# Reciprocal roots of the first norm and of the indexer key's norm: a power on GpSimd and one Newton step in place of a seed and three steps

## The chip, the cores and the metric

The kernel runs on one core of a Trainium2 chip. The metric is the device time of one execution in microseconds (us). The engines of the core work side by side and meet at semaphores: TensorE (PE in the profile, its weight loads PEld) multiplies matrices, VectorE (DVE) and ScalarE (ACT) work element by element and can read the matmul results, GpSimd (POOL) works element by element on the on-chip memory alone, and SyncE (SP) issues most transfers.

## The reference

Two decoder layers over 512 tokens of width 1024, in float32. A layer norm stands in front of the layers. Each layer projects the tokens to the queries, keys and values of two attention groups (a sliding window of 128 with sinks, and a sparse one) and to an indexer that picks, for each query, the 128 best keys of the sparse group. The attention results are projected back, and a norm of the weighted sum follows; then a gated feed-forward block with a gated per-layer input, and a norm again.

What matters here is the layer norm:

```
mu  = x.mean(-1);  var = square(x - mu).mean(-1)
y   = (x - mu) * rsqrt(var + 1e-5) * g + b
```

It is computed on the input x (512 x 1024, "the first norm"), on the indexer's keys (512 x 32, once a layer, "the indexer key's norm"), and twice a layer on the residual stream.

## The kernel before

The tokens lie on the 128 partitions in four tiles (t = 0 to 3), each 128 x 1024. For a projection a tile is turned to features by TensorE transposes (L438); ScalarE copies the result to a high part `fh` (L440, reduced float32) and VectorE puts the rest in a low part `fl` (L441). Weights are split the same way: ScalarE makes the high part (L278), GpSimd subtracts it to get the low part (L279). A product is then three matmuls, high x high (L325), high x low of the weights (L326) and low x high (L327), summed in one bank.

The order of each engine's work is set by a planner: the framework simulates a timeline and gives each engine, at each moment, the earliest instruction in program order of those that are ready. `tc.issue_after(i)` adds the demand that what is traced in its block comes after instruction i on i's engine. Each engine then runs its list in that order.

The start-up works tile by tile. `ln_in(t)` is the first norm. Tile 0's mean and variance are VectorE's (L372, L392); for tiles 1 to 3 ScalarE sums the tile (L382), scales the sum (L383) and sums the squares (L377). VectorE subtracts the mean and multiplies by g (L397, two halves), takes the reciprocal root with `rstd_of`, and multiplies by it and adds b (L400, two halves). The program then turns the tile to features and projects it to the indexer's query, key and weights (`gi_out`, 296 columns). Beside this GpSimd and ScalarE build the tables of the rotary embedding: `rotary` reduces the angles in two passes, each with a rounding on GpSimd (L462, L463), products on ScalarE (L473) and subtractions on GpSimd (L477), six in the first pass and four in the second. The rotations (L511 on VectorE, L513 on GpSimd, then a split L516 and L517) need the tables.

`rstd_of` is VectorE's alone. L357 adds epsilon to the variance and scales it by -0.5, L358 makes a seed from the bits of the number, and three Newton steps follow, each with two operations for each column: L363 (t = s * s * v) and L364 (s = (t + 1.5) * s). For the first norm the operands are 128 x 1. For the indexer key's norm two token tiles go together (128 x 2): the scaling and the seed are one operation each, the steps are twelve. Its statistics are L562 and L563, its first fused operation L564, and L580 applies the root. The pair's keys are then rotated, split and transposed for the indexer's scores (L645), whose weighted sum VectorE makes (L648). The two norms on the residual stream use `rstd_of` too.

Of the kernel before, what the change touches and what calls it, by code (L numbers as in the profile page):

```python
# [10 lines left out]
F32 = mybir.dt.float32  # L11
# [4 lines left out]
OP = mybir.AluOpType  # L16
# [13 lines left out]
EPS = 1e-5  # L30
# [66 lines left out]
def hybrid_kernel(ctx: ExitStack, tc: tile.TileContext, x, p, positions, ln_in_g, ln_in_b, w_in,  # L97
# [3 lines left out]
    PE, V, A, G, SP = nc.tensor, nc.vector, nc.scalar, nc.gpsimd, nc.sync  # L101
# [6 lines left out]
    small = ctx.enter_context(tc.tile_pool(name="small", bufs=4))  # L108
# [10 lines left out]
    def slot(dt=F32R):  # L119
        return slots.tile([128, 512], dt, name="slot", tag="slot")  # L120

    def t2k(dt=F32):
        return tmp.tile([128, 512], dt, name="t2k", tag="t2k")

    def sm(n, name):
        return small.tile([128, n], F32, name=name, tag=name)
# [222 lines left out]
        return slice(t * 128, (t + 1) * 128)  # L349


    def rstd_of(var, n=1, of=1):

        v = sm(n, f"lnv{n}")
        s = sm(n, f"lns{n}")
        t = sm(n, f"lnt{n}")
        V.tensor_scalar(v, var, of * EPS, -0.5 / of, op0=OP.add, op1=OP.mult)  # L357
        V.tensor_scalar(s.bitcast(I32), v.bitcast(I32), -0.5, float(0x5F3759DF - 2 ** 30 - 2 ** 22),  # L358
                        op0=OP.mult, op1=OP.add)
        for _ in range(3):  # L360
            for i in range(n):
                c = slice(i, i + 1)
                V.tensor_scalar(t[:, c], s[:, c], s[:, c], v[:, c], op0=OP.mult, op1=OP.mult)  # L363
                V.tensor_scalar(s[:, c], t[:, c], 1.5, s[:, c], op0=OP.add, op1=OP.mult)  # L364
        return s

    stats, last = {}, {}

    def ln_stats(t, h):
        if h == 0:  # L370
            stats[t] = small.tile([128, 2, 6], F32, name="bst", tag="bst")
        V.bn_stats(stats[t][:, h, :], xt[t][:, h * 512:(h + 1) * 512])  # L372
# [13 lines left out]
    def ln_in(t):  # L386
        halves = [xt[t][:, h * 512:(h + 1) * 512] for h in range(2)]
        if t == 0:
            mv = sm(2, "bmv")
            for h in range(2):  # L390
                ln_stats(t, h)
            V.bn_aggr(mv, stats.pop(t))  # L392
            mean, var, of = mv[:, 0:1], mv[:, 1:2], 1
        else:
            (mean, var), of = stats.pop(t), D
        for h, c in enumerate(halves):
            V.scalar_tensor_tensor(c, c, mean, gb_in[h], op0=OP.add if t else OP.subtract, op1=OP.mult)  # L397
        rs = rstd_of(var, of=of)
        for h, c in enumerate(halves):
            last["norm"] = V.scalar_tensor_tensor(c, c, rs, gb_in[2 + h], op0=OP.mult, op1=OP.add).ins  # L400

# [46 lines left out]
    def split_bits(v, bits):  # L448
        e = math.floor(math.log2(abs(v)))
        q = 2.0 ** (e - bits + 1)  # L450
        return math.floor(v / q) * q

    def rotary():

        n = NT * 48
        ang, kk, aa = t2k(), t2k(), t2k()
        a3 = ang[:, :n].rearrange("p (t f) -> p t f", t=NT)
        G.tensor_tensor(a3, posf[:, :, None].to_broadcast([128, NT, 48]),
                        invf[:, None, :].to_broadcast([128, NT, 48]), OP.mult)
        magic = 1.5 * 2.0 ** 23  # L460
        for period, bits, terms in ((2 * math.pi * 4096, 7, 6), (2 * math.pi, 11, 4)):
            G.tensor_scalar(kk[:, :n], ang[:, :n], 1.0 / period, magic, op0=OP.mult, op1=OP.add)  # L462
            G.tensor_scalar(kk[:, :n], kk[:, :n], magic, 1.0, op0=OP.subtract, op1=OP.mult)  # L463
            rest = period
            products = []
            for i in range(terms):
                c = split_bits(rest, bits) if i < terms - 1 else float(np.float32(rest))
                rest -= c
                if i % 2 == 0:
                    pr = t2k()  # L470
                products.append(pr[:, i % 2 * n:i % 2 * n + n])
                with tc.issue_after(last["squares"]) if bits == 11 else nullcontext():
                    A.mul(products[-1], kk[:, :n], -c)  # L473
            if bits == 7:
                yield
            for pr in products:
                G.tensor_tensor(ang[:, :n], pr, ang[:, :n], OP.add)  # L477
        lim = 3.1415925
        G.tensor_scalar(ang[:, :n], ang[:, :n], lim, -lim, op0=OP.min, op1=OP.max)
        with tc.issue_after(last["squares"]):  # L480
            A.activation(aa[:, :n], ang[:, :n], AF.Sin)
            A.activation(kk[:, :n], ang[:, :n], AF.Sin, scale=0.5)
        G.tensor_tensor(kk[:, :n], kk[:, :n], kk[:, :n], OP.mult)
        G.tensor_scalar(kk[:, :n], kk[:, :n], -2.0, 1.0, op0=OP.mult, op1=OP.add)
        s3 = aa[:, :n].rearrange("p (t f) -> p t f", t=NT)
        c3 = kk[:, :n].rearrange("p (t f) -> p t f", t=NT)
        for tab, f0, h in ((tab64, 0, 32), (tab32, 32, 16)):
            A.copy(tab[:, :, 0, :h], c3[:, :, f0:f0 + h])
            A.copy(tab[:, :, 0, h:], c3[:, :, f0:f0 + h])
            A.copy(tab[:, :, 1, :h], s3[:, :, f0:f0 + h])  # L490
            G.tensor_scalar(tab[:, :, 1, h:], s3[:, :, f0:f0 + h], -1.0, 1.0, op0=OP.mult, op1=OP.mult)

    w_pump()
    ln_in(0)
    table = rotary()
    next(table)
    ln_in_sums(1)
# [21 lines left out]
    def turn(dst, src, n):  # L519

        ps = bank("tp", 2, F32R)
        for i in range(n):
            PE.transpose(ps[:, i * 128:(i + 1) * 128], src[:, i * 128:(i + 1) * 128], idr)  # L523
        A.copy(dst, ps[:, :n * 128])
# [23 lines left out]
    for l in range(L):  # L548
# [6 lines left out]
        def gi_out(t, ps):  # L555

            u = t % 2
            if u == 0:
                kin[t] = sm(2 * ID, "kin").rearrange("p (u d) -> p u d", u=2)
                kmv[t] = sm(4, "kmv").rearrange("p (u d) -> p u d", u=2)  # L560
            st = sm(6, "kst6")
            V.bn_stats(st, ps[:, 256:288])  # L562
            V.bn_aggr(kmv[t - u][:, u], st)  # L563
            V.scalar_tensor_tensor(kin[t - u][:, u], ps[:, 256:288], kmv[t - u][:, u, 0:1], ikg[:, l],  # L564
                                   op0=OP.subtract, op1=OP.mult)
            qs = []
            if t > 0:
                wi[t] = small.tile([128, IH], F32, name="wi", tag="wi", bufs=4)
                V.tensor_scalar(wi[t], ps[:, 288:296], IH ** -0.5 * ID ** -0.5, None, op0=OP.mult)
                qs = [slot(), slot()]  # L570
                r1 = ps[:, :256].rearrange("p (n d) -> p n d", n=IH)
                for j in range(2):
                    qv = qs[j].rearrange("p (n u s d) -> p n u s d", n=4, u=2, s=2)
                    rope(r1[:, 4 * j:4 * j + 4], t, 4, ID, qv[:, :, :, 0], qv[:, :, :, 1], 2, top=G.tensor_copy)
            if u == 1:
                t0 = t - 1
                kn, mv = kin[t0], kmv[t0]
                rs = rstd_of(mv[:, :, 1], 2)
                for i in range(2):
                    V.scalar_tensor_tensor(kn[:, i], kn[:, i], rs[:, i:i + 1], ikb[:, l], op0=OP.mult, op1=OP.add)  # L580
                ks = slot()
                iv = ks[:, :256].rearrange("p (t s u d) -> p t s u d", t=2, s=2, u=2)
                rope(kn, t0, 2, ID, iv[:, :, 0], iv[:, :, 1], 2, each=True, top=G.tensor_copy)

            def turns():
                if u == 1:
                    turn(kiT[:, t0 * 128:(t + 1) * 128], ks, 2)
                    ready.add(("ki", t0))
                for j, q in enumerate(qs):
                    qiT[t, j] = slot()  # L590
                    turn(qiT[t, j], q, 4)
                ready.add(("i", t))
                order.tick(0.6)
            order.later(D_GI if t < NT - 1 else D_KI, turns)
# [370 lines left out]
        for gi, fs in enumerate(GROUPS):  # L965
# [27 lines left out]
            for h in range(2):  # L993
                ps = [acc() for _ in range(NT)]
                n = len(hs)
# [72 lines left out]
```

## Time and profile before

| | us |
|---|---|
| median of 3 runs | 1251.45 |
| lowest and highest | 1251.43, 1251.7 |
| profiled execution | 1251.81 |
| its span, first to last instruction | 1249.7 |

| engine | busy us | share of the span |
|---|---|---|
| TensorE | 1225.9 | 98% |
| its weight loads | 1029.9 | 82% |
| VectorE | 765.2 | 61% |
| GpSimd | 682.9 | 55% |
| ScalarE | 576.4 | 46% |

A busy share is an average over the whole span; TensorE's is modelled, as matmuls overlap in its pipeline. A row of a timeline has its start in us from the span's start, its duration in us, engine, source line, operation, output and inputs with shapes, and how many like it were merged; in brackets stands the idle time of the engine before it and what ended it. Rows that overlap on one engine are pipelined.

### The profile page before, as it was taken

The page shows a single profiled execution, that of the slowest core. Times are in us where ns is not written, and L with a number is a line of the kernel's source. Part 1 is how long each engine was busy: PE and PEld are TensorE (multiplying, and loading weights), DVE is VectorE, ACT ScalarE, POOL GpSimd, SP SyncE. Part 2 cuts the span into 40 slices and gives each one's busy share as a digit, 9 for nine tenths or more (in the row PEclk, how much of TensorE's full clock was granted, in tenths as well). Part 3 has the DMA queues.
Part 4 walks back from the last instruction along what each step waited for, and adds up shares of the span by engine and source line. Part 5 has one row for each costly group of instructions (what it writes and reads, how often), then busy time and mean ns, then how long its engine had stood idle before and what let it go on. Part 6 is the DMA issues. An engine that isn't in the chain of part 4 may idle for free.

```text
span 1249.7 us, 18006 instructions
## 1 busy us (share of the span) xinstructions
PE 1225.9 (98%) x6552; PEld 1029.9 (82%) x6552; DVE 765.2 (61%) x1678; ACT 576.4 (46%) x1193; POOL 682.9 (55%) x555
## 2 busy tenths in 40 slices
PE   7999999999999999999999999999999999999996
PEld 5998777988888888888899987689888888888885
DVE  7699954682727272726677998286555555555365
ACT  6577763442434343433337787534343333333331
POOL 6885532566566666663169754234757575757400
PEclk9999999999999999999999999999999999999999
DMA  5232311333232323034033203114323333321321
GB/s 177 78 92 85 95 42 35 119 118 118 85 118 84 118 85 118 18 118 140 2 89 114 101 21 117 52 54 149 99 87 105 97 105 99 103 83 52 101 84 50
DMA packets 89264, 112.74 MB, mean 90 GB/s; under 512 B 5460, under 2 KB 66132, under 8 KB 89176
## 3 DMA queue, kind: packets, MB, share of 16 engines
q1 hardware_dynamic: 88504, 111.58, 28.5%
q8 instruction: 51, 0.84, 0.3%
q14 instruction: 37, 0.30, 0.1%
q10 hardware_dynamic: 672, 0.03, 0.0%
HBM read 109.49 MB, written 2.10 MB: 89 GB/s over the span
## 4 chain that ended last, share of the span: by engine, by line
PE 82%; POOL 5%; DVE 3%; issue 3%; ACT 3%; DMA 3%; SPq 0%; DVEq 0%; ACTq 0%; POOLq 0%
PE bank L325 24%; PE bank L326 24%; PE bank L327 24%; PE bank L715 3%; PE bank L684 3%; PE bank L721 2%; POOL wsp L279 2%; DMA wst<-in_w_pg_dram 2%; POOL wsp L257 1%; PE bank L523 1%; PE bank L438 1%; PE bank L732 1%; ACT wsp L278 1%; DVE slot L273 1%; POOL slot L517 1%
## 5 line engine op out<-in xcount | busy, mean ns | idle before, releaser
L279 POOL TENSOR_TENSOR wsp<-wst,wsp 128x1024 fp32r<-128x1024 f32 (+2 forms) x148 | 351.3, 2389 | 244.4 <-ACT wsp L278 240.8
L326 PE MATMUL bank<-fl,wsp 128*128 128x512 f32 (+1 forms) x768 | 284.8, 372 | 0.4 <-DVE fl L441 0.4
L325 PE MATMUL bank<-fh,wsp 128*128 128x512 f32 (+1 forms) x768 | 283.6, 372 | 1.0 <-ACT fh L440 1.0
L327 PE MATMUL bank<-fh,wsp 128*128 128x512 f32 (+1 forms) x768 | 283.1, 371 | 0.0
L278 ACT CAST wsp<-wst 128x1024 fp32r<-128x1024 f32 (+2 forms) x148 | 151.6, 1033 | 166.4 <-PE bank L327 126.2
L325 PE MATMUL bank<-wsp,fh 128*128 128x256 f32 (+3 forms) x512 | 165.2, 326 | 3.6 <-DVE work L648 2.0
L874 DVE TENSOR_TENSOR t2k<-bank,t2k 128x512 f32<-128x512 f32 x44 | 30.4, 692 | 222.0 <-PE bank L327 222.0
L326 PEld LDWEIGHTS bank<-fl,wsp 128*128 128x128 f32 x768 | 144.6, 188 | 25.7 <-DVE fl L441 0.9
L325 PEld LDWEIGHTS bank<-fh,wsp 128*128 128x128 f32 x768 | 143.6, 188 | 26.8 <-ACT fh L440 1.9
L327 PEld LDWEIGHTS bank<-fh,wsp 128*128 128x128 f32 x768 | 144.6, 188 | 24.9
L327 PE MATMUL bank<-wsp,fl 128*128 128x256 f32 (+3 forms) x512 | 163.7, 322 | 1.4 <-DVE fl L441 0.8
L326 PE MATMUL bank<-wsp,fh 128*128 128x256 f32 (+3 forms) x512 | 164.7, 322 | 0.0
L257 POOL TENSOR_TENSOR wsp<-slot,wsp 128x512 fp32r<-128x512 f32 x100 | 141.6, 1442 | 29.0 <-ACT wsp L256 29.0
L325 PE MATMUL bank<-wsp,slot 128*128 128x512 f32 x392 | 153.8, 392 | 0.0
L326 PE MATMUL bank<-wsp,slot 128*128 128x512 f32 x392 | 152.7, 390 | 0.0
L327 PE MATMUL bank<-wsp,slot 128*128 128x512 f32 x392 | 148.4, 390 | 0.0
L790 DVE TENSOR_TENSOR x<-bank,x 128x512 f32<-128x512 f32 x140 | 91.5, 684 | 88.5 <-PE bank L327 88.5
L904 ACT CAST slot<-t2k 128x256 fp32r<-128x256 f32 (+1 forms) x104 | 49.8, 497 | 144.1 <-DVE t2k L874 102.5
L257 POOL TENSOR_TENSOR wsp<-t2k,wsp 128x512 fp32r<-128x512 f32 x40 | 57.5, 1448 | 92.4 <-ACT wsp L256 92.4
L325 PEld LDWEIGHTS bank<-wsp,fh 128*128 128x128 f32 x512 | 97.6, 191 | 11.9 <-ACT fh L440 2.4
L327 PEld LDWEIGHTS bank<-wsp,fl 128*128 128x128 f32 x512 | 97.5, 191 | 7.9 <-DVE fl L441 1.1
L326 PEld LDWEIGHTS bank<-wsp,fh 128*128 128x128 f32 x512 | 98.0, 191 | 6.5 <-issue 1.2
(152 smaller groups left out, 2004.6 us busy)
## 6 DMA issues: line engine op xcount, KB each, us to landing
wst<-in_w_gu_dram SPq DMA_DIRECT2D x88, 512.0 KB, 3.5
slot<-in_w_down_dram SPq DMA_DIRECT2D x80, 256.0 KB, 2.8
wst<-in_w_in_dram SPq DMA_DIRECT2D x16, 512.0 KB, 3.6
wst<-in_w_o_dram SPq DMA_DIRECT2D x16, 512.0 KB, 3.8
wst<-in_w_pg_dram SPq DMA_DIRECT2D x16, 512.0 KB, 4.2
wst<-in_w_in_dram SPq DMA_DIRECT2D x8, 256.0 KB, 2.7
lng<-in_ln_g_dram SPq DMA_DIRECT2D x4, 512.0 KB, 4.8
lnb<-in_ln_b_dram SPq DMA_DIRECT2D x4, 512.0 KB, 5.5
```

The source lines that it names most:

```text
L257: G.tensor_tensor(w[:, 1, j], src[j], w[:, 0, j], OP.subtract)
L278: A.copy(w[:, 0, :a * n], st[:, :a * n])
L279: G.tensor_tensor(w[:, 1, :a * n], st[:, :a * n], w[:, 0, :a * n], OP.subtract)
L325: PE.matmul(o, sh, mh, start=start, stop=False, skip_group_check=again)
L326: PE.matmul(o, sh, ml, start=False, stop=False, skip_group_check=again)
L327: PE.matmul(o, sl, mh, start=False, stop=stop, skip_group_check=again)
L684: PE.matmul(ps[:, o:o + nn], qT[kind, t, g][:, j * 128:(j + 1) * 128], kT[c, s][:, k0:k0 + nn], start=(s == 0), stop=(s == 1))
L715: PE.matmul(o[u * 64:(u + 1) * 64], vt[b0 + b][:, c * 64:(c + 1) * 64], pts[b][:, u], start=b == 0, stop=b == nb - 1)
L721: PE.transpose(ps[:, j * 128:(j + 1) * 128], es[j][:, b * 128:(b + 1) * 128], idf)
L790: V.tensor_tensor(xt[t][:, c], ps, xt[t][:, c], OP.add)
L874: V.tensor_tensor(a, ps[1, f], a, OP.mult)
L904: A.copy(h[0], src)
```

## The change

A function `root_of` stands beside `rstd_of`, and the first norm (`ln_in`) and the indexer key's norm (`gi_out`) call it; the norms on the residual stream keep `rstd_of`. VectorE adds epsilon, GpSimd raises the result to the power of a constant tile of -0.5, and VectorE makes one Newton step. For one column the step is a multiply by -0.5 and the two operations of before; for two columns it is three operations on both columns at once, with tensors as operands. The six subtractions of the rotary reduction's first pass on GpSimd are held behind tile 0's power.

```
+    half = small.tile([128, 2], F32, name="half", tag="half", bufs=1)
+    G.memset(half, -0.5)
+
+    def root_of(var, n=1, of=1):
+
+        v = sm(n, f"lnv{n}")
+        s = sm(n, f"lns{n}")
+        t = sm(n, f"lnt{n}")
+        V.tensor_scalar(v, var, of * EPS, 1.0 / of, op0=OP.add, op1=OP.mult)
+        last["root"] = G.tensor_tensor(s, v, half[:, :n], OP.pow).ins
+        if n == 1:
+            V.tensor_scalar(v, v, -0.5, None, op0=OP.mult)
+            V.tensor_scalar(t, s, s, v, op0=OP.mult, op1=OP.mult)
+            V.tensor_scalar(s, t, 1.5, s, op0=OP.add, op1=OP.mult)
+        else:
+            V.tensor_tensor(t, s, s, OP.mult)
+            V.scalar_tensor_tensor(t, t, -0.5, v, op0=OP.mult, op1=OP.mult)
+            V.scalar_tensor_tensor(s, t, 1.5, s, op0=OP.add, op1=OP.mult)
+        return s
...
-        rs = rstd_of(var, of=of)
+        rs = root_of(var, of=of)
...
-            for pr in products:
-                G.tensor_tensor(ang[:, :n], pr, ang[:, :n], OP.add)
+            with tc.issue_after(last["root"]) if bits == 7 else nullcontext():
+                for pr in products:
+                    G.tensor_tensor(ang[:, :n], pr, ang[:, :n], OP.add)
...
-                rs = rstd_of(mv[:, :, 1], 2)
+                rs = root_of(mv[:, :, 1], 2)
```

## Rows read from the trace of the kernel before

**Rows 1.** The page: the span, and TensorE's busy time, share and instructions.
```profile
span 1249.7 us, 18006 instructions
PE 1225.9 (98%) x6552; PEld 1029.9 (82%) x6552; DVE 765.2 (61%) x1678; ACT 576.4 (46%) x1193; POOL 682.9 (55%) x555
```

**Rows 2.** Busy time of each engine by stage: PE, PEld, DVE, ACT, POOL; clock; DMA.
```profile
31.00:62.00 31.00, 29.54 (x204) 28.95 (x203) 20.75 (x73) 16.84 (x45) 27.12 (x39) 1.00 0.27 73
...
640.00:670.00 30.00, 28.64 (x197) 27.83 (x195) 19.32 (x69) 15.08 (x36) 24.85 (x37) 1.00 0.24 63
```

**Rows 3.** Waits of TensorE, 0 to 60 us: total, times, longest.
```profile
PE bank L327 <- DVE fl L441: 0.8, 1, 0.8
...
PE bank L327 <- DVE lns L358: 0.6, 1, 0.6
```

**Rows 4.** Timeline of VectorE, 8.5 to 12 us: the root of tile 0.
```profile
8.74 0.15 DVE L357 TENSOR_SCALAR lnv<-bmv 128x1 f32<-128x1 f32 x1
...
9.46 0.15 DVE L358 TENSOR_SCALAR lns<-lnv 128x1 int32<-128x1 int32 x1
9.64 0.27 DVE L363 TENSOR_SCALAR lnt<-lns,lnv 128x1 f32<-128x1 f32 x1
...
11.06 0.21 DVE L364 TENSOR_SCALAR lns<-lnt,lns 128x1 f32<-128x1 f32 x1
11.38 1.41 DVE L400 SCALAR_TENSOR_TENSOR x<-x,lns,bank 128x512 f32<-128x512 f32 x2
```

**Rows 5.** Timeline of ScalarE, 11 to 15 us.
```profile
11.77 0.67 ACT L278 CAST wsp<-wst 128x592 fp32r<-128x592 f32 x1
...
12.57 1.15 ACT L377 ACTIVATE t2k<-x,lnm 128x1024 bf16<-128x1024 f32 x1
...
13.72 1.05 ACT L440 CAST fh<-bank 128x512 fp32r<-128x512 f32 x2
```

**Rows 6.** Timeline of TensorE, 12 to 22 us: transposes, first matmuls, next transposes.
```profile
12.19 1.97 PE L438 MATMUL bank<-idf,x 128*128 128x128 f32 x8 [2.04 <-DVE x L400]
14.34 0.61 PE L325 MATMUL bank<-wsp,fh 128*128 128x296 f32 x1 [0.19 <-ACT fh L440]
...
15.97 0.61 PE L327 MATMUL bank<-wsp,fl 128*128 128x296 f32 x1 [0.77 <-DVE fl L441]
...
21.56 1.28 PE L438 MATMUL bank<-idf,x 128*128 128x128 f32 x8
```

**Rows 7.** Timeline of GpSimd, 5 to 31 us.
```profile
7.97 2.60 POOL L477 TENSOR_TENSOR t2k<-t2k 128x192 f32<-128x192 f32 x4 [0.48 <-ACT t2k L473]
10.54 2.06 POOL L279 TENSOR_TENSOR wsp<-wst,wsp 128x888 fp32r<-128x888 f32 x1
...
30.78 0.88 POOL L513 TENSOR_TENSOR t2k<-t2k 128x128 f32<-128x128 f32 x2 [3.77 <-DVE t2k L511]
```

**Rows 8.** Timeline of VectorE, 15 to 28 us: tile 0's low half, tile 2's second operation.
```profile
15.24 1.28 DVE L441 TENSOR_TENSOR fl<-bank,fh 128x512 fp32r<-128x512 f32 x2
...
26.11 1.40 DVE L400 SCALAR_TENSOR_TENSOR x<-x,lns,bank 128x512 f32<-128x512 f32 x2
```

**Rows 9.** GpSimd's instructions by form: busy us, mean ns, idle before and releaser.
```profile
L279 POOL TENSOR_TENSOR wsp<-wst,wsp 128x1024 fp32r<-128x1024 f32 x134 | 323.6, 2430 | 202.3 <-ACT wsp L278 198.7 <-DMA wst<-in_w_pg_dram 2.7
...
L695 POOL TENSOR_TENSOR ek<-sink,ng 128x4 f32<-128x4 f32 x16 | 3.2, 202 | 12.4 <-DVE ng L688 12.4
...
L463 POOL TENSOR_SCALAR t2k<-t2k 128x192 f32<-128x192 f32 x2 | 1.7, 862 | 0.2
...
L462 POOL TENSOR_SCALAR t2k<-t2k 128x192 f32<-128x192 f32 x2 | 0.7, 351 | 0.2
```

**Rows 10.** Timeline of VectorE, 652 to 657 us: the last key pair of layer 2.
```profile
652.51 1.25 DVE L357 TENSOR_SCALAR lnv<-kmv 128x2 f32<-128x2 f32 x1
...
656.34 0.91 DVE L580 SCALAR_TENSOR_TENSOR kin<-kin,lns,ikb 128x32 f32<-128x32 f32 x2
```

**Rows 11.** Timeline of GpSimd in the same stretch.
```profile
650.07 3.67 POOL L279 TENSOR_TENSOR wsp<-wst,wsp 128x768 fp32r<-128x768 f32 x2 [0.18 <-ACT wsp L278]
```

## The prediction

> **What bounds the kernel now.** I read the page's totals first, then busy time by stage, then what TensorE waited for, the chain of the first 60 us, and last the timelines of VectorE, ScalarE, GpSimd and TensorE around each root. The totals show TensorE busy for 98% of a span of 1249.7 us [rows 1]: nothing elsewhere costs time unless TensorE stands still for it. By stage the holes near the changed code are small: 1.46 us in 31 to 62 us and 1.36 us in 640 to 670 us [rows 2], the two places behind the indexer key's norms. The four roots of the first norm lie earlier, in the start-up, where TensorE is not fed yet. There two waits of 0.8 and 0.6 us are put down to VectorE [rows 3]: the low half of the features comes late because VectorE has something else in hand.
>
> Times are from one execution of 1251.81 us (span 1249.7 and 2.1 around it); the median of the runs is 1251.45, so I make the sum as a difference and take it from the median.
>
> **Token tile 0.** Before, the variance is scaled at 8.74, VectorE comes to the seed at 9.46, the three steps run from 9.64 to 11.27, 0.54 each, and the second fused operation (L400) begins at 11.38 [rows 4]. So VectorE pays 1.92 us from seed to L400, and two of three steps go: 2 x 0.54, with the hand-offs between them 1.1 us. The seed's place is taken by a multiply by -0.5 of the same form, so that costs nothing new. The power runs on GpSimd from 8.89 plus a hand-off of 0.1 (an estimate: the last step ends at 11.27, L400 begins at 11.38). GpSimd is idle then if the six subtractions of the rotary reduction, which began at 7.97, are held back, as the change does [rows 7].
>
> What the power costs no row shows. From below stands GpSimd's smallest TENSOR_TENSOR, 128x4, at 0.20 us; from above its dearest, 128x1024, at 2.43. Two TENSOR_SCALARs of one shape with other operations take 0.35 and 0.86, so an awkward operation can cost 2.5 times a plain one [rows 9]; 0.20 to 0.50 is nearest, and I take 0.35. Then it ends at 9.34 and is back at 9.44, before VectorE could use it (9.64). L400 begins at 10.28 instead of 11.38. The power has 0.20 us to spare before it delays anything, and 1.1 more before L400 is as late as now: the break-even price is 0.35 + 1.3, about 1.7 us.
>
> What that is worth is decided on ScalarE. TensorE's eight transposes begin at 12.19 and take 1.97, so the first bank of four is full near 13.2; but ScalarE has begun the squares of token tile 1 at 12.57, which hold it to 13.7, and copies that bank only at 13.72. The first matmul starts at 14.34; the third of its triple needs the low half and starts at 15.97 [rows 5, 6]. The subtraction that makes it begins only at 15.24, since VectorE takes tile 1's first fused operation ahead of it [rows 8]. With the norm 1.1 us earlier the first bank is full at 12.1, before ScalarE has ended the third weight copy (12.44) and before the squares can start. The copy stands behind the squares in the program, but it is ready first, so it can go at 12.5 and ends 0.6 later; the first matmul starts near 13.15. VectorE has nothing else then (its tile 1 work waits for the squares), so the low half takes 0.64 more (1.28 for two) and the third matmul starts near 13.8: 2.2 us earlier than now. If ScalarE keeps its order, it is 0. I take 2.2, because the copy is ready 0.5 us before the squares' turn.
>
> **Token tiles 1 to 3.** Each loses 1.1 us on VectorE, but its power stands in GpSimd's order between weight splits of about 2 us. The squares of tile 1 move up to 1.05 us back (two copies now before them) and end by 14.9, the fused pair takes 1.4, the power waits at most 2.06 (the longest split there, [rows 7]) and 0.35, the step 0.6: L400 by 19.3 at the latest, 17.0 at the earliest. TensorE wants its first half at 21.56 - 2.2 = 19.4, and that half ends 0.7 after L400 begins: between no delay and 0.6. I take 0.1. The wait of 0.6 us for tile 1's low half goes, since VectorE is ahead: -0.6. Tile 2's L400 began at 26.11 [rows 8]; the steps that go ahead of it (its own, tile 1's, most of tile 3's) are some 3.0 us, so with VectorE as full as before it begins near 23.1. A lead of 2.8 us is thus matched: no wait.
>
> **The rotary reduction** gives up a start at 7.97 for one near 9.4, and four powers stand among it: 1.4 + 3 x 0.35 = 2.5 us later for the tables. GpSimd then sat idle for 3.77 us until VectorE's first rotation at 30.8 [rows 7]; that idle time is the cover. Without it 2.5 us would land on the index queries. Cost taken: 0. The memset of the constant falls in idle time at the very start.
>
> **The indexer key's norm,** four pairs. In layer 2 the last pair takes VectorE from 652.51 to 656.34, of which the first scaling alone 1.25 us [rows 10]; it ends as GpSimd's weight splits end, at 653.74 [rows 11]. So a 128x2 operation of this form stood until GpSimd was done, where the 128x1 form takes 0.15. Afterwards: the same scaling, the power with two hand-offs (0.55), three small operations of about 0.25: near 655.1 (652.51 + 1.25 + 0.55 + 0.75), or 1.2 earlier. But if a split of 2.4 us goes ahead of the power it is 1.2 later. Between these ends I take +0.35 in all, for the one power in the stretch of layer 1 in which GpSimd is nearly full (27.1 of 31 us, [rows 2]). The Trainium skill, "Advanced Engine Details and Errata", section VectorE Performance Modes, says that VectorE's second port is shared with GpSimd, so that each blocks the other; the 1.25 us row agrees, and the three new operations have two SBUF inputs, which "GPSIMD Engine Reference", section 8, lists as contending too. By that rule each could stand for a split, and the pair would come out 2 us or more later instead of earlier.
>
> **Sum:** -2.2 - 0.6 + 0.1 + 0.35 = -2.35, so 1251.45 - 2.35, rounded to 1249.2 us.
>
> **Rivals.**
> *ScalarE's order stays.* The squares of tile 1 go first as now; the norm of tile 0 is early for nobody. For it: the chain runs through the squares, not through tile 0's root. Against: the copy is ready first. Only the 0.6 us wait goes: 1250.8.
>
> *The key norms give too.* If the powers find GpSimd free, the pairs end 1.2 us earlier in both layers, and some 0.9 of each hole [rows 2] closes on top of the forecast: 1247.4. Against: GpSimd is full there.
>
> *The power is dear (the other side).* Place: GpSimd, behind the scaling of tile 0 and in the full stretches of the last key pair. Point: 1.7 us for tile 0; for a pair, 1.2. At the upper bound of 2.43, tile 0 loses 0.7 and each of two pairs 1.2: 1251.45 + 3.1 = 1254.6. A first power that has to load code would be the same thing once: by 2.43 us of standing still plus 0.35, tile 0 is 1.1 us late, 1252.5. For the load speaks that the operation is new to the program; against it only that nothing of the kind shows on GpSimd in the trace of before. The Trainium skill, "GPSIMD Engine Reference", section 2.1, gives about 6 us for the first call of a freshly loaded kernel, with no instruction to be seen; by that tile 0 would be some 4.6 us late, an estimate of 1256. No row here shows such a load.
>
> **How the numbers follow.** Forecast 0.50, with 1248.0 to 1250.4 as its own range (the planner's order of ScalarE and of the later stages moves by an us or so); order stays 0.25; key norms too 0.12; dear power 0.13, of which the load is 0.04. A measurement of this kernel tells 0.2%, 2.5 us, from no change: faster is below 1248.95, slower above 1253.95. Half of the forecast and a little more (0.28) with the second rival (0.12) gives faster 0.40; the dear power gives slower 0.08; the rest, 0.52, is within. The range reaches from 1247.2 to 1252.4, which leaves out about one in ten below and one above.
>
> **What would show it.** Right: a power of 0.2 to 0.5 us near 9.0; L400 near 10.3; ScalarE's first feature copy before tile 1's squares; the first third-of-triple matmul near 13.8; no wait before tile 1's low half; then a constant lead of TensorE to the end. Wrong: the copy still after the squares (first rival), a power of over 1.7 us or a gap before it (the third), or a lead that is there at 30 us and gone at 60 or 670, behind the key pairs' powers.

## The result and the profile after

| | before | after |
|---|---|---|
| median, us | 1251.58 (1251.23 to 1252.53, 6 runs) | 1259.38 (1259.05 to 1259.61, 6 runs) |
| ratio, 95% interval | | 1.0060 (1.0050 to 1.0071) |
| profiled execution, its span | 1251.81, 1249.7 | 1259.05, 1257.3 |

The change makes the kernel 7.8 us slower. The forecast was 1249.2 us with a range up to 1252.4, so the time lies above the range. The totals of the page after, against [rows 1]:

```profile
span 1257.3 us, 17956 instructions
PE 1229.2 (98%) x6552; PEld 1033.8 (82%) x6552; DVE 753.5 (60%) x1622; ACT 577.7 (46%) x1193; POOL 687.2 (55%) x564
```

VectorE is 11.7 us less busy and the kernel is 7.6 us longer: a first sign that nothing was bound by VectorE's sum. Where the time goes shows best as a lead: the start of one and the same VectorE operation (the key's statistics, the sums of the norms) in a kernel minus its start before, at six places of the span before (a minus sign means earlier). The last key pair of layer 1 lies between the columns of 39 and 203 us, that of layer 2 between 637 and 813.

| us later than before, at | 22 | 39 | 203 | 637 | 813 | 1241 |
|---|---|---|---|---|---|---|
| the changed kernel | -1.1 | +0.4 | +4.2 | +4.0 | +7.5 | +7.6 |

The start-up is nearly even, the long stretches of TensorE's work change nothing, and 3.8 and 3.5 us are lost behind the last pair of each layer. The first pairs (tiles 0 and 1), in the same code, cost nothing.

The column at 39 us needs care. It is the start of tile 3's statistics, and TensorE has by then done a different number of the next projection's matmuls of 384 columns: 16 before, 14 in the changed kernel, 11 to 24 in the experiments. Each takes 0.17 us at full pace. Put at the number of before, the changed kernel is 0.8 us late at 39 and loses 3.4 behind layer 1's last pair. Figures put so are called "at equal work" below. At 637 us TensorE has done the same number in every kernel.

The two stages by engine, after, to be laid beside [rows 2]:

```profile
31.00:62.00 31.00, 28.24 (x180) 27.82 (x179) 14.02 (x41) 14.97 (x33) 24.91 (x38) 0.94 0.20 52
...
640.00:670.00 30.00, 26.44 (x170) 25.95 (x169) 15.29 (x55) 9.41 (x22) 21.67 (x37) 0.94 0.19 53
```

TensorE's holes grew from 1.46 and 1.36 us to 2.76 and 3.56, and its clock, 1.00 before, is 0.94. The list of its waits names the reason: two are on the index score's sum (L669), which lies behind the pair's keys; one, in layer 1, is on GpSimd itself (L538). The waits on L420 and L461 are the start-up's.

```profile
PE bank L325 <- DVE work L669: 3.3, 1, 3.3
...
PE bank L458 <- DVE x L420: 2.7, 2, 1.6
...
PE bank L327 <- DVE fl L461: 1.8, 1, 1.8
PE bank L666 <- DVE work L669: 1.7, 1, 1.7
...
PE bank L544 <- POOL slot L538: 1.0, 1, 1.0
```

GpSimd and VectorE in the last pair of layer 2, in order of time, which answer to [rows 11] and [rows 10] (lines after the new function are 20 or 21 higher; L361 is the power, L367 to L369 the step on two columns, L601 the scaling of the keys):

```profile
655.58 0.73 POOL L538 TENSOR_TENSOR slot<-t2k,slot 128x256 fp32r<-128x256 f32 x1
...
656.20 0.16 DVE L360 TENSOR_SCALAR lnv<-kmv 128x2 f32<-128x2 f32 x1
656.28 4.19 POOL L279 TENSOR_TENSOR wsp<-wst,wsp 128x768 fp32r<-128x768 f32 x2
660.42 0.88 POOL L534 TENSOR_TENSOR t2k<-t2k 128x128 f32<-128x128 f32 x2
661.26 0.70 POOL L361 TENSOR_TENSOR lns<-lnv,half 128x2 f32<-128x2 f32 x1
...
662.00 0.33 DVE L367 TENSOR_TENSOR lnt<-lns 128x2 f32<-128x2 f32 x1 [5.64 <-POOL lns L361]
...
663.38 0.41 DVE L601 SCALAR_TENSOR_TENSOR kin<-kin,lns,ikb 128x32 f32<-128x32 f32 x2
```

The variance is scaled at 656.36. The power that needs it takes 0.70 us, but GpSimd has begun two weight splits (4.19) just before and does two of the rotation's products next, so it starts 4.90 later. VectorE, which runs its list in order, waits 5.64 us with the rotation and the index scores behind it. From scaling to the end of L601 it takes 7.59 us; before, it took 4.74 (652.51 to 657.25, [rows 10]). What TensorE makes of that:

```profile
664.90 0.44 PE L325 MATMUL bank<-wsp,fh 128*128 128x384 f32 x1 [3.33 <-DVE work L669]
665.18 0.34 PE L326 MATMUL bank<-wsp,fh 128*128 128x384 f32 x1
665.36 0.34 PE L327 MATMUL bank<-wsp,fl 128*128 128x384 f32 x1
...
666.29 0.52 PE L325 MATMUL bank<-wsp,fh 128*128 128x384 f32 x1
666.61 0.52 PE L326 MATMUL bank<-wsp,fh 128*128 128x384 f32 x1
...
669.17 0.34 PE L325 MATMUL bank<-wsp,fh 128*128 128x384 f32 x1
```

The same stretch by its totals (the last three columns are granted clock, DMA share, GB/s):

```profile
664.90:669.20 4.30, 4.30 (x16) 4.30 (x17) 2.27 (x6) 2.61 (x10) 4.16 (x10) 0.60 0.00 0
```

TensorE stands 3.33 us, and a little after it starts again ten of its matmuls come 0.32 apart instead of 0.17: 10 x 0.15 = 1.5 us more, at a granted clock of 0.60 over these 4.3 us. In the same stretch of before (640 to 685 us) TensorE's waits on the score's sum and behind it were shorter:

```profile
PE bank L325 <- DVE work L648: 1.0, 1, 1.0
PE bank L325 <- ACT slot L613: 0.6, 1, 0.6
```

So 3.3 - 1.6 + 1.5 = 3.2 of the 3.5 us lost are named. Layer 1 has the same picture: the power whose input is there at 41.27 starts at 46.89, TensorE waits 1.02 and 1.74 us, and ten matmuls come at half pace. With every wait of TensorE from the pair on, those on the attention's operands too, the sums close: 4.0 us against 2.1 before in layer 1 (39 to 203 us) and 4.8 against 2.8 in layer 2 (637 to 820), and with 1.5 of half pace in each that is 3.4 and 3.5 us.

### The profile page after: what moved, and what is told of

The parts are those of the page before. It is cut to its first block, busy times and chain, and to the rows that moved or that the text cites. A ratio compares the mean times of both kernels' runs of the same rounds, so it can differ in the third digit from the quotient of the medians.

```text
span 1257.3 us, 17956 instructions
## 1 busy us (share of the span) xinstructions
PE 1229.2 (98%) x6552; PEld 1033.8 (82%) x6552; DVE 753.5 (60%) x1622; ACT 577.7 (46%) x1193; POOL 687.2 (55%) x564
## 4 chain that ended last, share of the span: by engine, by line
PE 88%; POOL 3%; DVE 2%; issue 2%; ACT 2%; DMA 2%; SPq 0%; DVEq 0%; POOLq 0%; ACTq 0%
PE bank L325 26%; PE bank L327 25%; PE bank L326 25%; PE bank L705 3%; PE bank L736 3%; PE bank L742 2%; POOL wsp L279 2%; DMA wst<-in_w_pg_dram 1%; PE bank L544 1%; PE bank L458 1%; DVE slot L273 1%; PE bank L666 1%; PE bank L753 1%; DMA wst<-in_w_in_dram 1%; ACT t2k L744 0%
## 5 line engine op out<-in xcount | busy, mean ns | idle before, releaser
L325 PEld LDWEIGHTS bank<-wsp,fh 128*128 128x128 f32 x512 | 99.1, 194 | 11.9 <-DVE work L669 3.7
L326 PEld LDWEIGHTS bank<-wsp,fh 128*128 128x128 f32 x512 | 99.1, 194 | 5.7 <-issue 0.4
```

Of the source, the lines that this page charges most:

```text
L325: PE.matmul(o, sh, mh, start=start, stop=False, skip_group_check=again)
L326: PE.matmul(o, sh, ml, start=False, stop=False, skip_group_check=again)
```

## Experiments

Each ran in five rounds, 5 to 11 executions, beside the kernel before on the same chip (medians of before 1251.92, 1251.89 and 1251.90 for the three groups). Leads at the places of the table above, ratio with its 95% interval:

| | 22 | 39 | 203 | 637 | 813 | 1241 | us | ratio |
|---|---|---|---|---|---|---|---|---|
| e1_first_norm_only | -1.0 | +2.2 | +2.8 | +2.7 | +2.6 | +3.2 | 1254.53 | 1.0019 (1.0010 to 1.0028) |
| e2_key_norm_only | -0.4 | -0.4 | +3.0 | +3.5 | +7.0 | +7.2 | 1259.08 | 1.0056 (1.0043 to 1.0068) |
| e3_power_ahead | -1.1 | +0.4 | +1.7 | +1.8 | +3.3 | +3.5 | 1255.24 | 1.0033 (1.0021 to 1.0045) |
| e4_multiply | -1.3 | +2.3 | +3.6 | +3.8 | +5.2 | +5.1 | 1257.15 | 1.0043 (1.0031 to 1.0056) |
| e5_tile0_only | -0.8 | +1.1 | +2.0 | +2.0 | +3.7 | +4.0 | 1256.75 | 1.0039 (1.0026 to 1.0052) |
| e7_first_pairs_only | -1.0 | +1.1 | +0.9 | +0.9 | +0.3 | +0.5 | 1251.48 | 0.9998 (0.9989 to 1.0006) |
| e8_ahead_by_column | -1.0 | +1.0 | +2.9 | +3.4 | +4.3 | +4.5 | 1255.90 | 1.0035 (1.0022 to 1.0047) |
| e11_tile0_low_first | -2.3 | -0.8 | -0.6 | -0.6 | -0.0 | +0.2 | 1251.81 | 1.0002 (0.9993 to 1.0011) |
| e12_low_first_seed_by_column | -2.4 | -0.5 | 0.0 | 0.0 | +0.2 | +0.2 | 1251.76 | 1.0001 (0.9991 to 1.0010) |
| e13_tiles_0_2_3 | -2.3 | -1.2 | +0.5 | +0.4 | +0.4 | +0.4 | 1252.35 | 1.0003 (0.9995 to 1.0012) |
| e14_first_norm_low_first | -1.8 | -1.2 | +0.4 | +0.4 | +0.4 | +0.8 | 1252.55 | 1.0007 (0.9998 to 1.0017) |
| e15_power_unread | -0.4 | -0.4 | +0.5 | +0.6 | +1.7 | +1.9 | 1253.35 | 1.0013 (1.0004 to 1.0022) |

At equal work the column at 39 reads +2.0 in e1, +0.8 in e3 and e4, +1.6 in e5, +1.5 in e7, +0.9 in e8, -0.2 in e11, +0.4 in e12, -0.7 in e13 and e14; e2 and e15 are unchanged.

**One half at a time: e1, e2, e7.** In all three the edit is against the changed kernel.

```
e1 (first norm alone)
-                rs = root_of(mv[:, :, 1], 2)
+                rs = rstd_of(mv[:, :, 1], 2)
e2 (key norm alone)
-        rs = root_of(var, of=of)
+        rs = rstd_of(var, of=of)
-            with tc.issue_after(last["root"]) if bits == 7 else nullcontext():
+            with nullcontext():
e7 (all but the last pairs)
-                rs = root_of(mv[:, :, 1], 2)
+                rs = (root_of if t < NT - 1 else rstd_of)(mv[:, :, 1], 2)
```

> Only the first norm uses the power; the indexer key's norm keeps seed and three steps. Theory A (the power of the last key pair stands on GpSimd behind weight splits, VectorE behind it, TensorE behind both, 3.8 us in each layer): the loss in both layers goes, the 0.4 us lost up to 40 us stays, 1251 to 1252.5 us. Rival B (the power is dear: 0.55 to 0.71 us each against the 0.35 forecast, eight of them): half the loss stays, near 1255.5. Rival C (the start-up with its four powers costs the time): 1258 to 1259.5, as with the whole change.

> Only the indexer key's norm uses the power; the first norm keeps seed and three steps, and the rotary subtractions are not held. Theory A (queue of the last pair's power): 1258 to 1260 us, and in the trace the last pair's power starts 5 us or more after its scaling in both layers. Rival B (price of the power): near 1255.5. Rival C (start-up): 1251 to 1252.

> The changed kernel, but the last key pair of each layer has the seed and three steps again; the first norm and the first pairs keep the power. Theory A (nearly all of the loss stands behind the power of the last pair, which waits for splits on GpSimd): the last pairs' 7 us go, what is left is the start-up's +0.4 to +2.2: 1252 to 1254. Rival (the first pairs' powers or the start-up carry a part that only shows later): over 1255.

e2 has the whole loss of the pairs, as theory A said: +3.4 behind layer 1's last pair, +3.5 behind layer 2's, the power starting 5.6 and 4.9 us after its input and TensorE again standing 3.3 us on L669. e1 fits no theory's range. Without a power in any pair it is 3.2 us late at the end, and 2.0 of that, at equal work, is there at 39 us, in a start-up with the same code as the changed kernel's (+0.8); this is taken up below. e7 is the cleanest statement: one condition that keeps the power out of the last pair of each layer takes the kernel from a ratio of 1.0060 to 0.9998 (1251.48 us, a little under theory A's range). Its last pair of layer 2 (VectorE):

```profile
653.28 1.74 DVE L378 TENSOR_SCALAR lns<-lnv 128x2 int32<-128x2 int32 x1
...
656.91 0.91 DVE L601 SCALAR_TENSOR_TENSOR kin<-kin,lns,ikb 128x32 f32<-128x32 f32 x2
```

The seed and three steps, the long way, have the keys scaled at 657.82, where the short way with the power has them at 663.79 (3.1 us of that is the lead of after at that place): the arithmetic that was removed cost less than the place in GpSimd's list. The first pairs, with the power, cost nothing: in layer 2 GpSimd has been idle there for 9.35 us until the rotation comes.

**The price or the place: e4, e15.**

```
e4 (against the changed kernel)
-        last["root"] = G.tensor_tensor(s, v, half[:, :n], OP.pow).ins
+        last["root"] = G.tensor_tensor(s, v, half[:, :n], OP.mult).ins
e15 (against the kernel before; half and G.memset(half, -0.5) added)
                 rs = rstd_of(mv[:, :, 1], 2)
+                G.tensor_tensor(sm(2, "unread"), mv[:, :, 1], half, OP.pow)
```

> The whole change with the power replaced by a multiplication on GpSimd of the same shape, so that the roots are not computed; what is queued before the last pair's instruction stays. Theory A (queue): the instruction takes 0.2 instead of 0.55 to 0.71 us and starts as late as the power did: 1257.5 to 1259 us. Rival B (the power's price): 1251 to 1253 us.

> The kernel before with four more operations: a power of two columns on GpSimd at each key pair, into a tile that nothing reads; all roots are the seed and three steps. It prices the power's place on GpSimd without anyone waiting for it. Theory A (the loss is VectorE's wait behind the list): at most 0.7 us for each last pair, 1251.5 to 1253. Rival B (the power's own time and port, or what it moves in GpSimd's list, are the loss): 2 us or more behind each last pair, 1255 or above.

The multiply leaves the roots uncomputed. It takes 0.20 us instead of 0.70, starts at the same place in the list, and in layer 2 TensorE stands 2.81 us instead of 3.33. The half pace does not come there; the first matmul behind the wait, and the window that answers to the one above:

```profile
664.18 0.45 PE L325 MATMUL bank<-wsp,fh 128*128 128x384 f32 x1 [2.81 <-DVE work L669]
```

```profile
664.90:669.20 4.30, 4.30 (x27) 4.30 (x26) 2.27 (x6) 2.51 (x10) 3.75 (x10) 1.00 0.01 4
```

27 matmul records lie in these 4.3 us against 16 above. So the power's own 0.5 us did not cost 0.5 but 2 us in layer 2 (+3.5 against +1.4, one trace of each): it lengthened a standstill after which the clock fell. In layer 1 of e4 the half pace does come (granted clock 0.56 from 51.2 to 54.8 us), behind a wait of 2.4 us, and the pair costs 2.9 at equal work against 3.4. The time, 1257.15, is just under theory A's range: with a multiply in the power's place the last pairs still cost 4.3 of their 6.9 us. The power without a reader (e15) costs 0.9 and 1.1 us in the two layers: somewhat over the 0.7 that theory A allowed (its 1253.35 us is just past that range), and far under 3.5. Most of the loss is the wait for it, not its presence.

**Out of the list: e3, e8.**

```
e3 (against the changed kernel: two later splits held behind the last pair's power)
-                yield from project(ws, 296, (t,), from_f, done, 3 * (t == 3))
+                yield from project(ws, 296, (t,), from_f, done, 1 * (t == 3))
+            with tc.issue_after(last["root"]):
+                w_rel()
+                w_rel()
e8 (e3, and the two-column step by columns)
-            V.tensor_tensor(t, s, s, OP.mult)
-            V.scalar_tensor_tensor(t, t, -0.5, v, op0=OP.mult, op1=OP.mult)
-            V.scalar_tensor_tensor(s, t, 1.5, s, op0=OP.add, op1=OP.mult)
+            for i in range(n):
+                c = slice(i, i + 1)
+                V.tensor_scalar(v[:, c], v[:, c], -0.5, None, op0=OP.mult)
+                V.tensor_scalar(t[:, c], s[:, c], s[:, c], v[:, c], op0=OP.mult, op1=OP.mult)
+                V.tensor_scalar(s[:, c], t[:, c], 1.5, s[:, c], op0=OP.add, op1=OP.mult)
```

> The whole change, but two of the three weight splits that follow the last tile's projection to the indexer are put behind the last key pair's power on GpSimd, in both layers. Theory A: the power starts within 1 us of its scaling (near 41.5 and 653 us instead of 46.9 and 661.3), the 3.8 us a layer go: 1250.5 to 1252.5 us, and TensorE keeps its full pace near 52 and 666 us. Rival B (price) and rival C (start-up): 1257.5 to 1259.5, since neither the power's price nor the start-up changes.

> As the kernel with two splits behind the last pair's power, and the Newton step of a pair is done column by column with pointer scalars, so that no VectorE operation of it reads two tensors. Theory P (what is left of the loss in a last pair, 1.3 to 1.5 us a layer, is the step's L367 and L368, which ended with a GpSimd split at 1.77 and 2.32 us): each of the column operations takes 0.1 to 0.2 us, the turn's rotation follows 2.5 to 3 us earlier, and a last pair costs 0 to 0.5: 1252 to 1253. Theory Q (what is left is the splits themselves, which TensorE then waits for about 1 us, and what lies behind them): the step is short, but the lead still grows by 1 or more a layer, 1254 to 1255.5.

In e3 the power starts 1.47 us after its input in layer 1 and 0.75 in layer 2, and more than half of each layer's loss goes (+1.3, at equal work +0.9, and +1.5 are left). So its 1255.24 us lies between the ranges of theory A and of its rivals: the list explains the larger part, not all. A second stall appears in the same rows (GpSimd and VectorE, in order of time):

```profile
654.89 0.70 POOL L361 TENSOR_TENSOR lns<-lnv,half 128x2 f32<-128x2 f32 x1
655.56 4.17 POOL L279 TENSOR_TENSOR wsp<-wst,wsp 128x768 fp32r<-128x768 f32 x2
...
655.62 1.77 DVE L367 TENSOR_TENSOR lnt<-lns 128x2 f32<-128x2 f32 x1 [1.48 <-POOL lns L361]
657.42 2.32 DVE L368 SCALAR_TENSOR_TENSOR lnt<-lnt,lnv 128x2 f32<-128x2 f32 x1
```

L367 and L368 touch two numbers per partition and last 1.77 and 2.32 us: the second ends at 659.74, as GpSimd's pair of splits does (659.73). The prediction had named such a stall for the new step, with a split for each operation; two of the three show it. The Trainium skill, "SBUF — State Buffer", section "SBUF: two separate sides", calls the port pair that VectorE and GpSimd share a lock held for a whole instruction; these two ends agree with it. e8 takes the two-tensor operations out of the step, and it runs unhindered, but the next operation with two tensors inherits the stall:

```profile
657.55 0.46 DVE L370 TENSOR_SCALAR lnt<-lns,lnv 128x1 f32<-128x1 f32 x2
657.92 0.33 DVE L371 TENSOR_SCALAR lns<-lnt,lns 128x1 f32<-128x1 f32 x2
658.17 3.32 DVE L603 SCALAR_TENSOR_TENSOR kin<-kin,lns,ikb 128x32 f32<-128x32 f32 x2
```

Theory P falls as it was put: the step is short, the time is no better (1255.90, a little over theory Q's range too). In both kernels TensorE now also waits for a split itself, 1.0 us in e3:

```profile
PE bank L326 <- POOL wsp L279: 1.0, 1, 1.0
```

So GpSimd owes both in this stretch, and whichever goes second is late.

**The start-up: e5, e11, e13, e14.** Key pairs as before in all four.

```
e5 (power for tile 0 alone)
-        rs = root_of(var, of=of)
+        rs = (root_of if t == 0 else rstd_of)(var, of=of)
e11 (e5, and VectorE's order held)
+        with tc.issue_after({2: last.get("norm"), 3: last.get(("low", 1))}[t]) if t > 1 else nullcontext():
+            for h, c in enumerate(halves):
...
-            V.tensor_tensor(fl[:, 4 * j:4 * j + 4, ts], pv, fh[:, 4 * j:4 * j + 4, ts], OP.subtract)
+            last["low", t] = V.tensor_tensor(fl[:, 4 * j:4 * j + 4, ts], pv, fh[:, 4 * j:4 * j + 4, ts], OP.subtract).ins
e13 (e11, power for tiles 0, 2 and 3); e14 (e11, power for all four)
```

> The power stays in tile 0's root alone; tiles 1 to 3 and the key pairs have the seed and three steps again. The key pairs are then those of before, so the lead of the VectorE events should not change after 40 us. Theory A (GpSimd's list in tiles 1 to 3 holds their powers up, and so the start-up loses what tile 0 wins): the lead stays at -1 to -2 us from 20 us to the end, 1249.5 to 1250.5. Theory C (once tile 0 is early, tile 1's steps are late in VectorE's own order, behind tile 2's deviations and tile 3's, and TensorE, which has run out, comes back at its half pace): TensorE stands twice for 1.5 to 2 us between 18 and 24 as in the kernel with the power in the first norm, and the lead is +0.4 to +2.6 at 40 us and keeps it, 1252 to 1254.5.

> The power in tile 0's root alone, and VectorE's order is held: tile 2's deviations and root come after tile 1's normalised halves, tile 3's after tile 1's low half. Theory C (the start-up's loss is VectorE's order): TensorE's two waits between 18 and 24 shrink under 0.8 us each, the pace does not fall again after them, and the lead is -1.5 to -3 at 40 us and keeps it: 1248.5 to 1250. Rival (VectorE has too much to do for tiles 1 to 3 in that time whatever the order, and the wait goes over to tile 2 or 3): the lead is -0.5 to +1.5 at 40: 1251 to 1253.

> Key pairs as before; the power in the first norm for tiles 0, 2 and 3 (not 1, whose power stood behind splits), with VectorE's order held as in the kernel with tile 0 alone. VectorE, without a pause between 14 and 34 us there, has six small operations less for each of two tiles, some 0.9 us each. Theory V (VectorE's work is what the start-up is bound by once tile 0 is early): tiles 2 and 3 are normalised 0.5 to 1.5 us earlier than with tile 0 alone, the lead is -1 to -2.5 at 40 us, 1249.5 to 1251. Rival (GpSimd's list holds these powers up as well, or TensorE waits for something else): the lead is no better than -0.8, 1251 to 1252.5.

> Key pairs as before, the power in the first norm for all four tiles, with VectorE's order held (tile 2 behind tile 1's normalised halves, tile 3 behind tile 1's low half). Against the kernel with the power in the whole first norm and the planner's own order, +2.2 at 40 us. Theory C (order): the lead falls to between -1.5 and +0.5 at 40 us: 1250 to 1252. Theory A (tile 1's power behind GpSimd's splits, at about 17.4, is what holds the start-up): tile 1's halves come at 19.4 as there, TensorE waits 1.5 to 2 us for them, and the lead stays +1 to +2.5: 1252.5 to 1254.

e5 has no power in tiles 1 to 3 and loses there what e7 loses with one in each (+1.6 and +1.5 at equal work): TensorE waits 2.3 us for tile 1's halves and 1.3 for its low half. Its time, 1256.75, is above both ranges, in part because of layer 2 (below). Theory A does not hold for the start-up; the planner, with tile 0 early, puts tile 2's and tile 3's deviations ahead of tile 1's last steps and low half. e11 shows that by undoing it: the waits shrink to 0.7 and 0.8. The clock moves with it. By stage, 26 to 30 us, e1:

```profile
26.00:30.00 4.00, 4.00 (x19) 3.98 (x18) 2.18 (x7) 1.92 (x5) 3.15 (x8) 0.50 0.05 17
```

and e11:

```profile
26.00:30.00 4.00, 2.69 (x18) 2.02 (x18) 4.00 (x15) 2.91 (x11) 2.54 (x7) 1.00 0.02 4
```

The clock goes with what is lost by 39 us at equal work: over 22 to 30 us it is 0.58 in e1 (+2.0), 0.57 in e5 and e7 (+1.6, +1.5), 0.79 in the changed kernel and in e4 (+0.8 both), 1.00 in e11 and e13 (-0.2, -0.7). Only e14, with 0.80 and -0.7, stands apart. But e11 keeps only -0.8 of its -2.3, at equal work -0.2: the row above has VectorE busy for the whole 4.00 us, tile 2's halves begin at 25.70 against 26.11 before [rows 8], and TensorE waits 1.49 us for the first of them, which ends at 26.44 (the profile itself names no releaser). So theory C has the cause of what e5 lost, and the rival what is left then: the wait goes over to tile 2, and the time is the rival's (1251.81). e13 was to relieve VectorE there and fails by the mechanism of the last pairs: tile 2's power is ready at 21.1 and runs at 23.84, behind a split, and the halves begin at 25.59, 0.1 earlier than in e11. In e14 tile 1's halves begin at 18.70 us, against 18.19 in e11 and 19.41 in the changed kernel, so tile 1's power costs 0.5 and the order 0.7. TensorE waits 1.5 and 0.9 us there, and still the lead at 39 us is -1.2 as in e13 (-0.7 at equal work), against theory A. At 203 us both leads are gone (+0.5 and +0.4), behind a pair without a power; by its time alone, 1252.55, e14 would count for theory A. No version tried is faster than the kernel before by more than its interval.

**The seed by column: e12.** (e11, with the scaling and the bit operation of a pair written per column.)

```
+        for c in (slice(i, i + 1) for i in range(n)):
+            V.tensor_scalar(v[:, c], var[:, c], of * EPS, -0.5 / of, op0=OP.add, op1=OP.mult)
...
```

> As the kernel with the power in tile 0 alone and VectorE's order held, and the seed of a key pair (scaling and bit operation on 128x2) done column by column. Theory P (a VectorE operation on two columns waits for GpSimd's operation to end, one on a single column does not: 1.25 us for L357 in the last pair of layer 2 before): the pair's root is 0.5 to 1.5 us shorter in each last pair, and the lead falls by 0 to 1 in each layer: 1247 to 1249.5. Rival (what TensorE waits for behind the pair is not VectorE's root but GpSimd's split): the root is shorter but the lead stays within 0.3 of the kernel beside it.

```profile
652.30 0.14 DVE L378 TENSOR_SCALAR lnv<-kmv 128x1 f32<-128x1 f32 x1
...
655.00 2.42 DVE L534 TENSOR_TENSOR t2k<-kin,tab 128x128 f32<-128x128 f32 x1
```

The scaling of the later tile's column takes 0.14 instead of 1.25 [rows 10] and its root ends at 654.31 instead of 656.42, but the rotation behind it then lasts 2.42 us, about to the end of GpSimd's split. From 203 us on the lead is 0.0 to +0.2, no better than e11's -0.6 to +0.2, and the time is the same: theory P falls, and the rival fits.

**What stays open.** The planner orders the later instructions anew from its own costs whenever one changes. So last pairs without a power gain or lose too: at equal work -0.6 in each layer of e7, +1.2 and +1.1 in layer 1 of e13 and e14, +1.7 in layer 2 of e5. e5's pair there has the operations of before at the same distances; of TensorE's waits from 637 to 820 us, 3.7 against 2.8, 1.5 against 0.2 lie on ScalarE in the attention (L736), behind the pair. So the 0.9 and 1.5 us that e3 keeps, e4's 1.4 in layer 2 and e15's 1 us can't be divided between mechanism and order. The order of before was not pinned in any run.

## Why the prediction was wrong

**The step that failed is the key pair's term,** "+0.35 in all, for the one power in the stretch of layer 1 in which GpSimd is nearly full". It measured +3.8 and +3.5: with 7.0 us it is the larger part of the 10.2 us missed; 3.1 more are the start-up's, forecast at -2.7 and measured at +0.4. (At equal work the pairs are +3.4 and +3.5, the start-up +0.8.) The working named the mechanism ("if a split of 2.4 us goes ahead of the power it is 1.2 later") and was wrong on three points. First, the list: not one split but two, and two products, went ahead, 4.9 us of waiting; the row that the term rests on [rows 11] ends at 653.7 us, and what GpSimd had queued behind it entered only as one split of 2.4. The same timeline of before, read on, shows more:

```profile
653.70 0.73 POOL L517 TENSOR_TENSOR slot<-t2k,slot 128x256 fp32r<-128x256 f32 x1
654.39 2.40 POOL L279 TENSOR_TENSOR wsp<-wst,wsp 128x1024 fp32r<-128x1024 f32 x1
656.74 0.88 POOL L513 TENSOR_TENSOR t2k<-t2k 128x128 f32<-128x128 f32 x2
```

A power whose input is there at 653.76 would have had its turn behind these three rows at 657.6, 3.9 us later (an estimate that takes this order as it stands). Second, who waits: in order behind VectorE's L367 stand the rotation and the index scores, which TensorE needs. Third, the pace: a standstill of 3.3 us was followed by 1.5 us of slowed matmuls, which no term had.

The stall that the prediction named beside this term, an operation with two tensors standing for a split, is not what the changed kernel lost by: its three new operations took 0.33, 0.30 and 0.65 us in layer 2, and the longest in layer 1 took 1.35. It came in e3 and e8, once the power was early. Two slips in the numbers change nothing: -2.35 gives 1249.1, not 1249.2, and more than half of the forecast was put below 1248.95, a bound that lies under the forecast itself.

**The rival "power dear"** had the right place and the wrong price: it counted the power's duration, 1.2 us a pair at 2.43 us. The duration is 0.70; the wait is 4.9. Its chance of 0.13 stood on the price, so the chance of slower was far too small.

**The power's price** was 0.55 to 0.58 us for one column and 0.70 to 0.71 for two, over the 0.35 taken and well within the bounds; the first one, at 8.99, lasts no longer than the others. The load that the Trainium skill, "GPSIMD Engine Reference", section 2.1, gives for the first call of a freshly loaded kernel does not show. For tile 0 the price hardly mattered, as worked out: L420 came 0.15 late.

**Tile 0** came as forecast to 0.2 us (power, L420 on VectorE; the copy ahead of the squares on ScalarE; the first and the third matmul on TensorE), against [rows 4 to 6]:

```profile
8.99 0.58 POOL L361 TENSOR_TENSOR lns<-lnv,half 128x1 f32<-128x1 f32 x1 [1.43 <-DVE lnv L360]
...
10.43 1.41 DVE L420 SCALAR_TENSOR_TENSOR x<-x,lns,bank 128x512 f32<-128x512 f32 x2
...
12.52 0.56 ACT L460 CAST fh<-bank 128x512 fp32r<-128x512 f32 x1
12.98 1.15 ACT L397 ACTIVATE t2k<-x,lnm 128x1024 bf16<-128x1024 f32 x1
...
13.13 0.62 PE L325 MATMUL bank<-wsp,fh 128*128 128x296 f32 x1
...
13.86 0.61 PE L327 MATMUL bank<-wsp,fl 128*128 128x296 f32 x1
```

The rival of an unchanged ScalarE order is refuted. The 2.1 us won here are gone by 39 us.

**Tiles 1 to 3** were costed at +0.1 and a wait that goes, -0.6. L420 of tile 1 came at 19.41, 0.1 past the latest forecast, and TensorE waited twice, 3.4 us in all, where 0.1 was costed:

```profile
17.36 0.57 POOL L361 TENSOR_TENSOR lns<-lnv,half 128x1 f32<-128x1 f32 x1
...
20.21 1.38 PE L458 MATMUL bank<-idf,x 128*128 128x128 f32 x8 [1.59 <-DVE x L420]
...
23.95 0.54 PE L327 MATMUL bank<-wsp,fl 128*128 128x296 f32 x1 [1.76 <-DVE fl L461]
```

The sentence that failed is "VectorE is ahead": TensorE, earlier and at full pace, ended tile 0's projection at 18.6, and VectorE was full. e5 and e11 put this mainly on VectorE's order, and e14 leaves 0.5 us for tile 1's power. The rotary tables were covered, as said: GpSimd's idle time before the first rotation shrank from 3.77 to 0.69 us. The test named last in the prediction, a lead "that is there at 30 us and gone at 60 or 670", came in by half: time is lost behind the key pairs' powers, but the lead was gone by 39 us, before them.

## What to carry to other kernels

An operation given to another in-order engine costs its place in that engine's list at the moment its input is ready, not its duration: read that list, from that moment on, for every place of the edit, and in the fullest stage first. Then ask what stands in order behind the instruction that waits. A lead won at the start is worth only what the next shared engine leaves of it.

## What the hardware showed that was not expected

A standstill of TensorE cost more than its length here: after 3.33 us its matmuls of 384 columns came 0.32 apart for 3.2 us (granted clock 0.60 over the stretch, the lower of its two levels, 1.2 GHz, in most of it); after 2.81 us in the same place they came 0.17 apart at 1.00. The length alone does not decide it: in layer 1 of the changed kernel standstills of 1.02 and 1.74 us, with 0.9 us of work between them, were followed by the same half pace. A VectorE operation on two columns lasted 1.77 and 2.32 us beside GpSimd's splits, where one-column operations took 0.14 to 0.28; taken out of one instruction, the stall went to the next with two tensors (3.32 us for two such, 2.42 for one).
